# Stick-breaking attention on one core: steps taken in pairs, with the PSUM banks shared out anew

## The chip, the cores and the metric

The kernel runs on one core of a Trainium2 chip. The metric is the device time of one launch in microseconds (us), lower is better. A core has TensorE (PE, with its weight loads as PEld), VectorE (DVE), ScalarE (ACT), GpSimd (POOL) and SyncE (SP, whose queue issues all DMAs here). The TensorE clock has two levels, 1.2 and 2.4 GHz. PSUM is used as eight banks of 128 x 512 float32.

## What is computed

One sequence of 1024 tokens, width 1024, float32, goes through a Mamba-2 layer, a projection to shared K and V, and a stick-breaking attention layer, with a final norm. The change lies in the attention layer, whose reference is, for each of 16 heads of 64 columns and each block of 128 queries:

```python
z = einsum('bthd,bshd->bhts', q[:, lo:hi], k[:, :hi]) * scale
log_keep = where(mask, log_sigmoid(-z), 0)
after = cumsum(log_keep, reverse=True) - log_keep
a = exp(where(mask, log_sigmoid(z) + after, -inf))
o = einsum('bhts,bshd->bthd', a, v[:, :hi])
...
x = x + gate * ((o * silu(z_gate)) @ out_w)
```

The mask is strictly causal. `q` and `z_gate` are projections of the same normed stream, and `k`, `v` come from the stage before.

## The kernel before, in words

All earlier stages (Mamba-2, its output projection, K and V) end at about 982 us of the profile and aren't touched by the change, but for the pool of their projection banks. The attention stage works on eight head pairs `p`. PE's order there is written out by hand (`manual_schedule`, line 897); the other engines' orders are set by a planner, which sees each instruction's inputs and a priority in the order of the program.

**A step** is one row block `i` of 128 queries against up to 512 keys (`c` says which half of the keys), or two smaller ones side by side; nine steps (`order`, line 916) make a head pair, 72 the stage. A step has these parts:

- **S**, `scores` (line 824): six matmuls for each piece (three float32r products for each of two heads, on 64 rows each) into a tile `sc` of two banks. ACT makes two sigmoids of it (`kp` at 836, `be` at 837), POOL masks the diagonal block (843), DVE runs a product scan over `kp` for each head (850), POOL multiplies (856). `above` carries the scan from one half of the keys to the next.
- **T**, `transposes` (line 860): eight transposes of `be`, four for each head `a`, into one bank `at` for each head. ACT copies the first head's bank to SBUF (877), DVE the second's (875), into tiles `aT`.
- **A**, `av` (line 879): when both row blocks `2t` and `2t+1` have all their keys, the value products, 8 to 32 matmuls of up to 256 columns, into a bank `av`; DVE multiplies it with the gate (890).
- **F**, the filler: units of three 512-column matmuls (`mm3`) of the projections of the gates (`zproj1`, 16 units for each head pair) and of the next pair's queries (`qproj`, 16 units), then of the output projections (`oproj`, 7 units each), into one bank `mm` for eight (seven) units. Each bank is then emptied: for queries by a cast on ACT (772) and a subtraction on DVE (773), for gates by a sigmoid (787) and a product (788), for `oproj` by one DVE instruction (801). `load_w` (116) loads each weight tile, casts it on ACT (123) and subtracts on POOL (124).

Before the change, a step of the main loop (line 922) emits T of the step three earlier (`LAG`), then half of its filler units (`rates`, 2 to 4 for a step), then any A that became ready a step earlier (`AVD`), S of the new step, and the other half of the filler. The banks: two `mm`, two for `sc`, two `at`, one `av`, one for a constant. `mm` is a pool of the whole kernel. Four filler units of pair 0's gates run ahead of the loop, and output projections 0 to 5 are run with seven of their eight parts, the sixth left open in its bank until the last stage.

Of the kernel before, what the change touches and what calls it, by code (L numbers as in the profile page):

```python
# [31 lines left out]
LAG = 3  # L32
AVD = 1
NPRE = 5
# [18 lines left out]
def tile_trunk(ctx, tc, xT, xN, c, vec, ada0, adar, wxbc, wwave, wdt, wz, wmo, wk, wv, wq, wqz, wso, out):  # L53
# [37 lines left out]
    pmm = pool(ctx, "pmm", bufs=2, space=PSUM)  # L91
# [6 lines left out]

    esw = ctx.enter_context(ExitStack())
# [13 lines left out]
    def mm_tile(name):  # L113
        return pmm.tile([P, HT], F32, tag="mm", name=name)
# [626 lines left out]
    esw.close()  # L741
    weight_pools(ctx, 1, 2, 2)
    pg = pool(ctx, "pg", bufs=2)
    gg, x2p, part = [{}, {}], [], {}
# [12 lines left out]
    with ExitStack() as es:  # L757
        pa = pool(es, "p5", bufs=2)
        pp = pool(es, "pp5", bufs=2, space=PSUM)
        pone = pp.tile([P, 1], F32, name="pone", bufs=1)  # L760
# [16 lines left out]
        def zproj1(p):  # L777
            wh, wl = load_w(wqz[p], f"qz{p}", parts=4, eng=Q)
            szs[p] = [None] * NH
            for hf in (1, 0):  # L780
                sz = pa.tile([P, HT], F32, tag="sz", name=f"qsz{p}_{hf}", bufs=3)
                szs[p][hf] = sz
                ps = mm_tile(f"pqz{p}_{hf}")
                for k in range(ND):
                    mm3(ps, wh[:, k, :], wl[:, k, :], *h1[k][hf], k == 0, k == ND - 1)
                    if k == ND - 1:
                        S.activation(sz, ps, AF.Sigmoid)
                        V.tensor_tensor(out=sz, in0=ps, in1=sz, op=ALU.mult)
                    yield

        def oproj(d):
            if d < NPRE:
                t = pg.tile([P, HT], F32, tag="x2", name=f"x2_{d}", bufs=NPRE)
                Y.dma_start(out=t, in_=x1_d[d][1])
                x2p.append(t)
            wh, wl = load_w(wso[d], f"so{d}", parts=4, eng=Q)
            ps = mm_tile(f"pso{d}")
            for k in range(7):
                mm3(ps, wh[:, k, :], wl[:, k, :], *gg[1][k], k == 0, k == 6 and d < NPRE)
                if k == 6 and d < NPRE:  # L800
                    V.scalar_tensor_tensor(out=t, in0=ps, scalar=mod[:, GA1, d:d + 1], in1=t,
                                           op0=ALU.mult, op1=ALU.add)
                yield
            part[d] = ps, wh, wl
# [19 lines left out]
        def scores(p, step):  # L824
            kd, q = pairs[p][0], qs[p]
            n = f"{p}_{step[0][0]}_{step[0][1]}"
            kp = pa.tile([P, 2, HT + 2], F32, tag="kp", name="kp" + n)
            be = pa.tile([P, 2, HT], F32, tag="be", name="be" + n, bufs=4)
            ps = pp.tile([P, 2, HT], F32, tag="sc", name="sc" + n, bufs=1)
# [30 lines left out]
        def transposes(p, step, be):  # L860
            n = f"{p}_{step[0][0]}_{step[0][1]}"
            for a in range(2):
                ps = pp.tile([P, 4, P], F32, tag="at", name=f"at{n}_{a}", bufs=2)
# [39 lines left out]
        def filler():  # L903
# [6 lines left out]
            for d in range(NPRE + 1):  # L910
# [10 lines left out]
        live, rows, ready = {}, {}, []  # L921
        for n in range(len(steps) + LAG + AVD):
            rate = rates[n % ns]
            m = n - LAG
            now, ready = [r for r in ready if r[0] <= n], [r for r in ready if r[0] > n]
            if 0 <= m < len(steps):
                p, st = steps[m]
                transposes(p, st, live.pop(m))
                for i, c in st:
                    if i % 2 == 1 and c == 0:  # L930
                        ready.append((n + AVD, (p, i // 2, rows.pop((p, i // 2)))))
            for _ in range((rate + 1) // 2):
                next(fl, None)
            for r in now:
                av(*r[1])
            if n < len(steps):
                p, st = steps[n]
                if n % ns == 0:
                    if p < 7:
                        pairs[p + 1] = load_pair(p + 1)  # L940
                live[n] = scores(p, st)
            for _ in range(rate // 2):
                next(fl, None)
# [4 lines left out]
    with ExitStack() as es:  # L948
        pw = pool(es, "p6w")
        pf = pool(es, "p6", bufs=2)  # L950
        pp = pool(es, "pp6", bufs=2, space=PSUM)
        wos = {}
# [17 lines left out]
        keep_w(NPRE + 1)  # L970
# [3 lines left out]
        for hf, c0, c1, ds in ((1, 0, 512, (0, 5, 1, 2, 3, 4, 6, 7)), (0, 0, 256, (6, 7, 0, 1, 2, 3, 4, 5)),  # L974
# [10 lines left out]
            for i, d in enumerate(ds):  # L985
# [8 lines left out]
                if hf == 1 and d == NPRE:  # L994
                    ps = part[d][0]
                elif hf == 1 and d < NPRE:
# [5 lines left out]
                elif hf == 1 and d == NPRE:  # L1002
                    mm3(ps, part[d][1][:, 7, :], part[d][2][:, 7, :], *gg[1][7], False, True)
# [103 lines left out]
```

## Time and profile before

| | us |
|---|---|
| median of 3 runs | 1463.79 |
| lowest and highest | 1463.76, 1465.89 |
| the profiled execution | 1468.16 |
| its span, first to last instruction | 1465.3 |
| attention stage, from the first score matmul to the last transpose | 987 to 1376 |

Engines over the whole span: PE 98%, PEld 77%, DVE 66%, ACT 50%, POOL 36%. PE's busy time is from start to a modelled end, and neighbouring matmuls overlap, so a PE that is always busy can still lose time at the places where one kind of matmul follows another: there the distances from start to start tell more than the busy time.

### The profile page before, as it was taken

How to read it: one execution, taken by the hardware profiler on the slowest of the kernel's cores; microseconds unless marked ns; L12 is line 12 of the kernel's file. 1: busy time of each engine (PE TensorE's matmuls, PEld its weight loads, DVE VectorE, ACT ScalarE, POOL GpSimd, SP SyncE). 2: the span in 40 equal slices, each digit the busy share in tenths (PEclk: the TensorE clock that was granted, in tenths of full speed). 3: DMA queues.
4: the chain of work that ended last, by engine and by line, in shares of the span. 5: the costliest groups of instructions: out<-in, count | busy, mean ns of one | idle time of the engine just before them, and what ended most of it. 6: DMA issues, size and time to landing. Idle time of an engine off the chain costs nothing.

```text
span 1465.3 us, 20960 instructions
## 1 busy us (share of the span) xinstructions
PE 1431.0 (98%) x7772; PEld 1125.0 (77%) x7772; DVE 965.4 (66%) x1212; ACT 734.8 (50%) x1234; POOL 521.8 (36%) x602
## 2 busy tenths in 40 slices
PE   6998999999999999999999999999999999999997
PEld 3777887888777777778888888887777777777797
DVE  5689984544799888985733627516666666667674
ACT  6654535234666666633522424326555555556452
POOL 0011221001555655431011000027666666667532
PEclk9999999999999999999999999999999999999999
DMA  9368875224577766557433546561222121212253
GB/s 355 127 215 300 293 292 178 101 89 142 172 239 237 233 221 216 191 188 276 156 129 112 197 143 214 168 207 38 80 63 75 58 73 59 71 58 80 92 184 113
DMA packets 105445, 235.75 MB, mean 161 GB/s; under 512 B 9344, under 2 KB 40832, under 8 KB 103296
## 3 DMA queue, kind: packets, MB, share of 16 engines
q1 hardware_dynamic: 105344, 234.42, 47.4%
q8 instruction: 61, 1.00, 0.3%
q14 instruction: 40, 0.33, 0.1%
HBM read 188.51 MB, written 45.88 MB: 160 GB/s over the span
## 4 chain that ended last, share of the span: by engine, by line
PE 80%; DVE 2%; DMA 1%; issue 1%; ACT 1%; POOL 0%; DVEq 0%; SPq 0%; POOLq 0%; ACTq 0%
PE av L886 5%; PE sc L833 4%; PE at L865 4%; PE pz L129 4%; PE pz L131 4%; PE pz L130 4%; PE po L131 4%; PE po L130 4%; PE po L129 4%; PE pq L129 2%; PE pqz L129 2%; PE yd L545 2%; PE pq L131 2%; PE pr L131 2%; PE pr L129 2%; PE pr L130 2%
## 5 line engine op out<-in xcount | busy, mean ns | idle before, releaser
L856 POOL TENSOR_TENSOR be<-be,kp 128x1024 f32<-128x1024 f32 (+2 forms) x96 | 163.1, 1699 | 83.1 <-DVE kp L850 73.9
L836 ACT ACTIVATE kp<-sc 128x1024 f32<-128x1024 f32 (+2 forms) x96 | 75.4, 813 | 149.5 <-PE sc L833 113.9
L850 DVE TENSOR_TENSOR_SCAN kp<-kp,pone 128x128 f32<-128x128 f32 (+3 forms) x128 | 96.7, 804 | 64.0 <-POOL kp L843 64.0
L129 PE MATMUL pr<-h0h,hx 128*128 128x512 f32 x336 | 132.6, 395 | 5.6 <-DVE cv L350 3.8
L131 PE MATMUL pr<-h0h,lx 128*128 128x512 f32 x336 | 132.2, 393 | 0.5 <-DVE lx L124 0.5
L130 PE MATMUL pr<-h0l,hx 128*128 128x512 f32 x336 | 132.1, 393 | 0.0
L129 PE MATMUL pz<-h0h,hz 128*128 128x512 f32 x256 | 112.9, 441 | 0.0
L130 PE MATMUL po<-yl,ho 128*128 128x512 f32 x256 | 100.9, 394 | 0.7 <-DVE yl L659 0.7
L131 PE MATMUL po<-yh,lo 128*128 128x512 f32 x256 | 100.0, 391 | 1.3 <-DVE lo L124 1.3
L131 PE MATMUL pz<-h0h,lz 128*128 128x512 f32 x256 | 100.3, 392 | 0.0
L130 PE MATMUL pz<-h0l,hz 128*128 128x512 f32 x256 | 100.0, 391 | 0.0
L129 PE MATMUL po<-yh,ho 128*128 128x512 f32 x256 | 100.0, 391 | 0.0
L515 ACT ACTIVATE lm<-lm,nac 128x128 f32<-128x128 f32 x256 | 78.6, 389 | 40.9 <-POOL lm L512 40.9
L363 POOL TENSOR_TENSOR ar<-ar,crow 128x1024 f32<-128x1024 f32 x12 | 31.0, 2587 | 184.5 <-DMA ar<-adar 157.0
L850 DVE TENSOR_TENSOR_SCAN kp<-kp,ab,pone 128x512 f32<-128x512 f32 x64 | 78.3, 1265 | 24.9 <-ACT kp L836 14.2
L124 POOL TENSOR_TENSOR lq<-rq,hq 128x256 fp32r<-128x256 f32 x32 | 22.5, 734 | 177.8 <-ACT hq L123 177.8
L550 POOL TENSOR_TENSOR sd<-st,eev 128x512 f32<-128x512 f32 x24 | 38.0, 1581 | 130.6 <-ACT st L562 117.9
L512 POOL TENSOR_SCALAR_AFFINE_SELECT lm<-lm 128x1024 f32<-128x1024 f32 x32 | 44.1, 1377 | 112.7 <-DMA lm<-ac_d 105.6
L350 DVE SCALAR_TENSOR_TENSOR cv<-pr,vt,cv 128x1023 f32<-128x1023 f32 (+2 forms) x63 | 80.2, 1276 | 0.9
L129 PEld LDWEIGHTS pr<-h0h,hx 128*128 128x128 f32 x336 | 63.7, 190 | 19.7 <-issue 4.2
L123 ACT CAST ho<-ro 128x1024 fp32r<-128x1024 f32 x32 | 33.6, 1052 | 85.0 <-PE po L130 66.9
L865 PEld LDWEIGHTS at<-ident,be 128*128 128x128 f32 x576 | 67.2, 140 | 10.6 <-DVE aT L875 0.8
(259 smaller groups left out, 3889.3 us busy)
## 6 DMA issues: line engine op xcount, KB each, us to landing
ar<-adar SPq DMA_DIRECT2D x48, 512.0 KB, 5.3
lm<-ac_d SPq DMA_DIRECT2D x32, 512.0 KB, 5.1
rz<-wz SPq DMA_DIRECT2D x32, 512.0 KB, 3.8
ro<-wmo SPq DMA_DIRECT2D x32, 512.0 KB, 3.7
xs_d<-sv SPq DMA_DIRECT2D x24, 512.0 KB, 3.7
rx<-wxbc SPq DMA_DIRECT2D x21, 512.0 KB, 4.5
a<-ada SPq DMA_DIRECT2D x8, 1024.0 KB, 10.1
xg<-xs_d SPq DMA_DIRECT2D x8, 1024.0 KB, 6.5
```

The lines of the kernel that those rows point to most:

```text
L129: E.matmul(ps, wh, xh, start=first, stop=False)
L130: E.matmul(ps, wh, xl, start=False, stop=False)
L131: E.matmul(ps, wl, xh, start=False, stop=last)
L350: V.scalar_tensor_tensor(out=ac[:, i:], in0=ps[:, :T - i], scalar=vv("cw", m * 4 + 3 - i), in1=ac[:, i:], op0=ALU.mult, op1=ALU.add)
L512: Q.affine_select(out=lm, in_=lm, pattern=[[0, HPG], [1, P]], compare_op=ALU.is_ge, fill=-1e30, base=0, channel_multiplier=-1)
L515: S.activation(lm[:, h, :], lm[:, h, :], AF.Exp, bias=nac[:, c, h0_ + h:h0_ + h + 1])
L833: E.matmul(ps[:, a, o:o + w], q[hsl[a], x, i * P:(i + 1) * P], kd[hsl[a], y, HT * c:HT * c + w], start=b == 0, stop=b == 2)
L836: S.activation(kp[:, :, ok:ok + w], ps[:, :, o:o + w], AF.Sigmoid, scale=-0.125)
L850: V.tensor_tensor_scan(out=ka, data0=ka, data1=pone.to_broadcast([P, w]), initial=1.0 if top else above[p, i][:, a, 0:1], op0=ALU.mult, op ...
L856: Q.tensor_tensor(out=be[:, :, o:o + w], in0=be[:, :, o:o + w], in1=kp[:, :, ok + 1:ok + w + 1], op=ALU.mult)
L865: E.transpose(ps[:, j, :], be[:, a, j * P:(j + 1) * P], ident)
L886: E.matmul(ps[hsl[a], cs], vd[:, j, hsl[a]], at[j // 4][:, a, j % 4, cs], start=j == 0, stop=j == nj - 1)
```

## The change

The loop takes two steps at a time. For pair `m` it emits T of step `2(m-2)`, four filler units, T of step `2(m-2)+1`, four filler units, every A that these two T completed, and then S of steps `2m` and `2m+1` back to back. Every ninth pair (`m % 9 == 8`) has no filler at all, and `m = 0` has none either. The bank shares become: one `mm` (a pool of the stage; the earlier and the last stage have their own with two), four for `sc` (two tiles), two `at` that T and A share, one constant. Output projections 0 to 5 all run with seven parts and are emptied; none is left open. The four filler units ahead of the loop fall away. `aT` becomes two tiles of each of two sizes, `sz` has four buffers, `kp` three.

```diff
-LAG = 3
-AVD = 1
-NPRE = 5
+LAG = 2
+NPRE = 6
...
-    pmm = pool(ctx, "pmm", bufs=2, space=PSUM)
+    pm = {}
...
+    esm = ctx.enter_context(ExitStack())
+    pm["mm"] = pool(esm, "pmm", bufs=2, space=PSUM)
...
     esw.close()
+    esm.close()
...
+        pm["mm"] = pool(es, "pmm5", bufs=1, space=PSUM)
...
-                sz = pa.tile([P, HT], F32, tag="sz", name=f"qsz{p}_{hf}", bufs=3)
+                sz = pa.tile([P, HT], F32, tag="sz", name=f"qsz{p}_{hf}", bufs=4)
...
-                mm3(ps, wh[:, k, :], wl[:, k, :], *gg[1][k], k == 0, k == 6 and d < NPRE)
-                if k == 6 and d < NPRE:
+                mm3(ps, wh[:, k, :], wl[:, k, :], *gg[1][k], k == 0, k == 6)
+                if k == 6:
...
-            ps = pp.tile([P, 2, HT], F32, tag="sc", name="sc" + n, bufs=1)
+            ps = pp.tile([P, 2, HT], F32, tag="sc", name="sc" + n)
...
-                        rows[p, t][c] = pa.tile([P, 2, 4, 256], F32, tag="aT", name=f"aT{p}_{t}_{c}",
-                                                bufs=4)
+                        nb = min(2 * t + 2 - 4 * c, 4)
+                        rows[p, t][c] = pa.tile([P, 2, nb, 256], F32, tag=f"aT{nb}",
+                                                name=f"aT{p}_{t}_{c}")
...
-            ps = pp.tile([P, 256], F32, tag="av", name=f"av{p}_{t}", bufs=1)
+            ps = pp.tile([P, 4, P], F32, tag="at", name=f"av{p}_{t}").rearrange("p a b -> p (a b)")[:, 0:256]
...
-            for d in range(NPRE + 1):
+            for d in range(NPRE):
                 yield from oproj(d)
...
-        for _ in range(4):
-            next(fl)
...
-        rates = (4, 4, 4, 4, 2, 4, 4, 3, 3)
...
-        for n in range(len(steps) + LAG + AVD):
-            rate = rates[n % ns]
-            m = n - LAG
...
+        for m in range(len(steps) // 2 + LAG):
+            ready = []
+            rest = 8 if m % ns != 8 else 0
+            for n in (2 * (m - LAG), 2 * (m - LAG) + 1):
+                if n >= 0:
+                    p, st = steps[n]
+                    transposes(p, st, live.pop(n))
+                    for i, c in st:
+                        if i % 2 == 1 and c == 0:
+                            ready.append((p, i // 2, rows.pop((p, i // 2))))
+                if m > 0:
+                    fill(rest // 2)
+            for r in ready:
+                av(*r)
+            for n in (2 * m, 2 * m + 1):
+                if n < len(steps):
+                    p, st = steps[n]
+                    if n % ns == 0 and p < 7:
                         pairs[p + 1] = load_pair(p + 1)
+                    live[n] = scores(p, st)
...
+        pm["mm"] = pool(es, "pmm6", bufs=2, space=PSUM)
```

## Rows read from the trace of the kernel before

**Rows 1.** The page: engines over the span, and the granted clock in 40 slices.

```profile
PE 1431.0 (98%) x7772; PEld 1125.0 (77%) x7772; DVE 965.4 (66%) x1212; ACT 734.8 (50%) x1234; POOL 521.8 (36%) x602
...
PEclk9999999999999999999999999999999999999999
```

**Rows 2.** Busy time, attention stage: stretch, then engine and count; clock, DMA, GB/s.

```profile
983.00:1379.00 396.00, 395.42 (x2573) 290.18 (x2573) 259.56 (x360) 225.61 (x383) 278.87 (x430) 1.00 0.22 71
```

**Rows 3.** Chain that ended last: first step of two successive head pairs (start, us).

```profile
1126.93 1.01 PE sc L833 x12
...
1175.54 1.01 PE sc L833 x12
```

**Rows 4.** Timeline of PE within a step: start, length, engine, line, tile.

```profile
1100.84 0.98 PE L833 MATMUL sc<-kd,q 64*128 64x256 f32 x12
1101.75 0.50 PE L129 MATMUL pq<-h1h,hq 128*128 128x512 f32 x1
...
1107.22 0.40 PE L131 MATMUL pq<-h1h,lq 128*128 128x512 f32 x1
1107.45 1.03 PE L865 MATMUL at<-ident,be 128*128 128x128 f32 x8
1108.24 0.47 PE L129 MATMUL pq<-h1h,hq 128*128 128x512 f32 x1
1108.56 0.39 PE L130 MATMUL pq<-h1l,hq 128*128 128x512 f32 x1
1108.79 0.40 PE L131 MATMUL pq<-h1h,lq 128*128 128x512 f32 x1
...
1109.48 0.40 PE L131 MATMUL pq<-h1h,lq 128*128 128x512 f32 x1
1109.81 0.96 PE L833 MATMUL sc<-kd,q 64*128 64x512 f32 x6
1110.70 0.50 PE L129 MATMUL pq<-h1h,hq 128*128 128x512 f32 x1
1111.04 0.39 PE L130 MATMUL pq<-h1l,hq 128*128 128x512 f32 x1
```

**Rows 5.** Timeline around a value product.

```profile
1114.55 3.46 PE L886 MATMUL av<-aT,vd 128*64 128x256 f32 x32
...
1117.93 0.54 PEld L833 LDWEIGHTS sc<-kd,q 64*128 64x128 f32 x6 [0.17 <-issue]
```

**Rows 6.** Timeline: a query bank filled and emptied.

```profile
977.18 0.39 PE L131 MATMUL pq<-h1h,lq 128*128 128x512 f32 x1
...
977.61 0.59 ACT L772 CAST q<-pq 128x512 fp32r<-128x512 f32 x1 [4.17 <-PE pq L131]
...
978.22 0.69 DVE L773 TENSOR_TENSOR q<-pq,q 128x512 fp32r<-128x512 f32 x1 [3.54 <-ACT q L772]
```

**Rows 7.** Timeline: an output projection's bank filled and emptied.

```profile
1385.76 0.39 PE L131 MATMUL pso<-gh,lso 128*128 128x512 f32 x1
...
1386.19 0.75 DVE L801 SCALAR_TENSOR_TENSOR x<-pso,mod,x 128x512 f32<-128x512 f32 x1 [0.46 <-PE pso L131]
```

**Rows 8.** Timeline: sigmoids of the S of rows 4, and copies after two T.

```profile
1102.56 1.03 PE L865 MATMUL at<-ident,be 128*128 128x128 f32 x8
...
1105.38 0.67 DVE L875 COPY aT<-at 128x512 f32<-128x512 f32 x1
...
1108.09 0.59 ACT L877 COPY aT<-at 128x512 f32<-128x512 f32 x1
...
1110.95 1.03 ACT L836 ACTIVATE kp<-sc 128x1024 f32<-128x1024 f32 x1 [2.27 <-POOL kp L847]
...
1111.33 0.66 DVE L875 COPY aT<-at 128x512 f32<-128x512 f32 x1
...
1111.87 1.02 ACT L837 ACTIVATE be<-sc 128x1024 f32<-128x1024 f32 x1
```

**Rows 9.** Groups by line and shape, attention stage: busy us, mean ns, idle before.

```profile
L850 DVE TENSOR_TENSOR_SCAN kp<-kp,ab,pone 128x512 f32<-128x512 f32 x64 | 78.3, 1265 | 24.9 <-ACT kp L836 14.2 <-POOL lqz L124 10.0 <-issue 0.2
...
L875 DVE COPY aT<-at 128x512 f32<-128x512 f32 x48 | 32.2, 672 | 16.4 <-PE at L865 16.2
```

**Rows 10.** Timeline: first query matmul, and the last V bank emptied.

```profile
971.42 0.39 PE L129 MATMUL pq<-h1h,hq 128*128 128x512 f32 x1
...
973.93 0.69 DVE L733 COPY vs<-pv 128x512 f32<-128x512 f32 x1 [2.98 <-DMA v_d<-vs]
```

More of the change, by code (lines that the diff above doesn't have):

```diff
@@ L113, in mm_tile @@
     def mm_tile(name):
-        return pmm.tile([P, HT], F32, tag="mm", name=name)
+        return pm["mm"].tile([P, HT], F32, tag="mm", name=name)
     def load_w(src, name, shape=(8, P), parts=1, eng=V):
@@ L741, in tile_trunk @@
     esw.close()
+    esm.close()
     weight_pools(ctx, 1, 2, 2)
     pg = pool(ctx, "pg", bufs=2)
-    gg, x2p, part = [{}, {}], [], {}
+    gg, x2p = [{}, {}], []
     def split_g(hf, k, g):
@@ L791, in oproj @@
         def oproj(d):
[L792 to L795, printed above, removed]
+            t = pg.tile([P, HT], F32, tag="x2", name=f"x2_{d}", bufs=NPRE)
+            Y.dma_start(out=t, in_=x1_d[d][1])
+            x2p.append(t)
             wh, wl = load_w(wso[d], f"so{d}", parts=4, eng=Q)
@@ L803, in oproj @@
                 yield
-            part[d] = ps, wh, wl
         def load_pair(p):
@@ L826, in scores @@
             n = f"{p}_{step[0][0]}_{step[0][1]}"
-            kp = pa.tile([P, 2, HT + 2], F32, tag="kp", name="kp" + n)
+            kp = pa.tile([P, 2, HT + 2], F32, tag="kp", name="kp" + n, bufs=3)
             be = pa.tile([P, 2, HT], F32, tag="be", name="be" + n, bufs=4)
-            ps = pp.tile([P, 2, HT], F32, tag="sc", name="sc" + n, bufs=1)
+            ps = pp.tile([P, 2, HT], F32, tag="sc", name="sc" + n)
             for i, c, w, o, _, _ in pieces(step):
@@ L862, in transposes @@
             for a in range(2):
-                ps = pp.tile([P, 4, P], F32, tag="at", name=f"at{n}_{a}", bufs=2)
+                ps = pp.tile([P, 4, P], F32, tag="at", name=f"at{n}_{a}")
                 for j in range(4):
@@ L909, in filler, with fill @@
                 load_gs(1, k)
-            for d in range(NPRE + 1):
+            for d in range(NPRE):
                 yield from oproj(d)
         fl = filler()
-        for _ in range(4):
-            next(fl)
+        def fill(m):
+            for _ in range(m):
+                next(fl, None)
         order = [((6, 1), (0, 0)), ((6, 0),), ((7, 1),), ((7, 0),), ((1, 0), (5, 1)), ((4, 1), (2, 0)),
                  ((4, 0),), ((5, 0),), ((3, 0),)]
-        rates = (4, 4, 4, 4, 2, 4, 4, 3, 3)
         ns = len(order)
         steps = [(p, st) for p in range(8) for st in order]
-        live, rows, ready = {}, {}, []
-        for n in range(len(steps) + LAG + AVD):
-            rate = rates[n % ns]
-            m = n - LAG
[L925 to L939, printed above, removed]
+        live, rows = {}, {}
+        for m in range(len(steps) // 2 + LAG):
[16 more added lines that the diff above has]
+                    if n % ns == 0 and p < 7:
                         pairs[p + 1] = load_pair(p + 1)
-                live[n] = scores(p, st)
-            for _ in range(rate // 2):
-                next(fl, None)
+                    live[n] = scores(p, st)
         for _ in fl:
@@ L968, in finish @@
                 yield
-        keep_w(NPRE + 1)
+        keep_w(6)
         keep_w(7)
@@ L993, in tile_trunk @@
                     Y.dma_start(out=t, in_=x1_d[d][hf][:, c0:c1])
-                if hf == 1 and d == NPRE:
-                    ps = part[d][0]
-                elif hf == 1 and d < NPRE:
+                if hf == 1 and d < NPRE:
                     ps = mm_tile(f"ps{d}_{n}")
@@ L1001, in tile_trunk @@
                     mm3(ps, w7[0][:, d, :], w7[1][:, d, :], *gg[1][7], True, True)
-                elif hf == 1 and d == NPRE:
-                    mm3(ps, part[d][1][:, 7, :], part[d][2][:, 7, :], *gg[1][7], False, True)
                 else:
```

## The prediction, made before the changed kernel was run

> **What bounds the kernel now.** I read the page first: PE is busy 98% of the span at full clock [rows 1]. Then the busy time of the attention stage alone: PE 395 of 396 us, DVE, ACT and POOL at 57 to 70% [rows 2]. So no engine but PE sets the pace there, and PE has no holes. The chain that ended last says the same with a period: a head pair starts every 48.61 us [rows 3], with no wait for another engine between. What remains to be won is in the distances from start to start, for which I read PE's timeline within a step [rows 4]. A filler matmul follows its like after 0.23 us. A gap above that belongs to the change from one kind of matmul to another:
>
> - F to S: 0.33 from the last filler matmul (1109.48) to S, so 0.10 lost.
> - S itself: six matmuls, in concurrent twos, are worth 3 x 0.23 = 0.69, but the filler starts 0.89 after S: 0.20 lost. The second filler matmul comes after 0.34: 0.11 more. S costs 0.41 in all at its two borders.
> - F to T: 0.23, nothing lost. T to F: 0.32 between the first two filler matmuls, 0.08 lost.
>
> The kernel loses 0.41 x 72 = 30 us to S, and that is what the change attacks. What it takes away to do so is slack: two projection banks, an A bank of its own, filler between any two T, and filler between S and T.
>
> **The gain.** Two steps before: 2 x 0.41 + 2 x 0.08 = 0.98. After: F to S once (0.10), S to S, S to T, T to F twice (0.16). S to S is shown nearly: S of two pieces, 12 matmuls of 256 columns, worth the same 0.69, lets the filler start after 0.91 [rows 4], so a second piece costs nothing at its border; I take 0, the bounds being 0 and 0.31. S to T isn't in the trace. Bounds: 0 (T behind F) and 0.31 (F behind S); I take 0.28, nearer the second, since what is lost behind S is S's own end. After: 0.54, so 0.44 saved for each of 36 pairs, 16 us (from 0.1 x 36 = 4 to 0.72 x 36 = 26). The Trainium skill, TensorEngine Tiling (Array Packing), Key Properties, says that a change of tiling mode, not of the tile, drains TensorE. By it S to S is free, and S (64 rows) to T (128) pays the drain, which is 16 us again and shuts out the 26. Value products: each A has 0.17 us of weight-load idling between itself and S [rows 5] on top of its own border; 32 of them become 24 groups, 8 x 0.2 = 1.6 us. **Gain: 17 us.**
>
> **One projection bank.** An emptied bank must be waited for wherever filler would go on. Filling a bank takes eight units, which are the two blocks of a pair, so its border falls behind the second block, and A, S, S, T (at least 0.69 x 2 + 0.28 + 0.8 = 2.5 us) hide the emptying, which takes 1.83 us when its engines are free: the cast starts 0.43 after the last matmul starts, the subtraction ends at 1.73 [rows 6], and 0.1 to restart. If a scan (1.27 us each) stands before the subtraction, the cover is gone and 0.4 to 1.6 is lost; I take none. Four places have no cover:
> - Pair 0's queries run ahead of the loop: between its halves 1.83 - 0.23 = 1.6 us.
> - The output projections have 7 units, so their borders fall inside filler. Five borders; the DVE step starts 0.43 after the last matmul and takes 0.75 [rows 7], 0.1 to restart, less 0.23: 1.05 each, **5 us**. Leaving none open for the last stage moves no matmul: the same three close it there.
> - The queries of pairs 2, 4, 6 end with the second block directly ahead of the S that reads them (no filler in the ninth pair, and no A there), as do pair 0's. S's second piece needs the half that was just emptied: 0.33 + 3 x 0.17 = 0.85 us after the last matmul it is due, the subtraction is there at 1.83: 1.0 each, **4 us**. For odd pairs an A and an S lie between.
> - The stage's bank may lie over a V bank, the last of which is emptied at 974.62, 3.2 us after the first query matmul [rows 10]. Between 0 and 3.2; the first two V banks are free before, so 0 is taken and 3.2 kept.
>
> **Two banks for T and A.** After S, S, T1 comes at 1.7 us from the first S, ends at 2.5, and four units later T2 is due at 5.3. Its banks need T1's copies. On ACT four sigmoids are ahead of the copy: the first starts 1.14 after S starts, the next 0.92 later [rows 4, 8], so the copy starts at 1.14 + 4 x 0.92 = 4.8 and ends at 5.4, plus 0.1: 0.2 late. On DVE the scans of both steps compete with it: two of 1.27 from 2.4 to 4.9, two more to 7.4 if the planner puts them first, then 0.67 for the copy [rows 9]. Before, the copy ended 2.70 and 3.75 us after the T [rows 4, 8]; now it has 3.2 (second half of T2). So a pair loses between 0 and 2.3 us. I take 0.35, ACT's 0.2 and a third of a pair's T in which DVE is half a microsecond late, as at 1111.33: 32 x 0.35 = **11 us** (0 to 74).
>
> **The ninth pairs** (m = 8, 17, 26, 35) have no filler: S, S, T1, T2, A, A, S, S. T2's first bank waits for T1's copy at 5.5, and T1 ended at 2.5: 3.0 us, and A for the banks after T2 about 0.2 more: 3.2 x 4 = **13 us**. If the copies went ahead of the sigmoids it would be 0.8 each (3 us), if behind all scans 5.5 (22 us).
>
> Other edits: `kp`, `sz` and `aT` have at least as many live tiles as the order needs, so no wait; SP issues the same loads (one `x1` load moves from the last stage into this one), POOL the same subtractions, both with ten microseconds of slack at a fifth of the DMA share [rows 2].
>
> **Sum:** -17 + 1.6 + 5 + 4 + 11 + 13 = +17.6 us. The profiled execution's own time is 1468.2, 0.3% above the median; a shift of 1% is the same on either. From the median 1463.8: **1481 us**.
>
> **Rivals.**
> 1. *The copies come in time* (faster). If the planner sets each T's two copies ahead of the second step's sigmoids and scans, the 11 go and the 13 become 3: -3 us. If S to T is also cheaper than taken, up to -13. It decides at the copy's end: under 3.2 us after T1. For it: DVE sat idle for T for 16.2 us in all [rows 9], so it does sometimes run the copy at once. Against: 3.75 us in rows where S wasn't even adjacent. Time 1457.
> 2. *The copies fall behind both scans in half of the pairs*: 16 x 2.3 in place of 11, and 22 in place of 13: +52, 1516 us.
> 3. *S to S costs as much as S to F*: the gain is 5, not 17: 1493.
> 4. *The clock falls.* Before, the clock stays at 1.00 all through the stage [rows 2], where the longest stretch without filler is A and S, 4.3 us [rows 4, 5]. The ninth pairs have some 11 us of T, waits, A and S. At 1.2 GHz their 8 us of matmuls would double: 4 x 8 = 32 us, 1513. The Trainium skill, TensorE: Matmul & The Clock Gate, Part 4, holds that transposes don't count as work for the clock; by that rule this is where it would fall, and no row here shows it.
>
> **How the numbers follow.** Forecast (all waits near what is taken) 0.60, rival 1 0.25, rival 2 0.08, rival 3 0.04, rival 4 0.03. A measurement of this kernel tells apart about 0.2%, 3 us. Of rival 1, 0.05 lies within 3 us, and of the forecast 0.03. Faster 0.20, same 0.08, slower 0.72. The likeliest's own range is 1470 to 1497. The range 1455 to 1500 leaves out rivals 2 and 4 and the lowest of rival 1, some 0.15.
>
> **What would show it.** Right: the granted clock 1.00; S to S start distance 0.69; PE idle before T on ACT and DVE `aT` copies, 4 large ones of 3 us and many under 1; PE idle before filler for L801, five times; the period of two head pairs 99 to 101 us where it was 97.2. Wrong: a period below 97, or T never waiting for a copy (rival 1), or T to F after S without the 0.2 to 0.3 of S's end.

## The result, and the profile after

The changed kernel takes **1504.18 us** (median, 1503.96 to 1507.27) where the kernel before took 1464.84 on the same chip: 1.027 times as long, interval 1.0253 to 1.0287. It is slower, as predicted, but by 39 us instead of 17.6, and 4 us above the top of the range. The profiled execution's span grew from 1465.3 to 1502.6.

The page's engine row and the busy time of the attention stage (columns as in [rows 1, 2]), for the changed kernel:

```profile
PE 1432.7 (95%) x7772; PEld 1134.1 (75%) x7772; DVE 962.9 (64%) x1213; ACT 734.2 (49%) x1234; POOL 513.7 (34%) x602
```

```profile
983.00:1414.00 431.00, 396.67 (x2591) 299.70 (x2590) 258.71 (x361) 224.42 (x380) 273.21 (x426) 0.98 0.20 65
```

Before, PE had 0.6 us of holes in 396 [rows 2]; now it has 34 in 431, and the mean granted clock of the stage is 0.98 instead of 1.00: 431 x 0.02 = 8.6 us, to the accuracy of that digit. Who owns the holes is told by the list of PE's waits (what PE waited at, on what; us in total, times, longest):

```profile
PE at L866 <- DVE aT L877: 22.9, 20, 2.8
PE pso L130 <- DVE x L803: 5.4, 3, 3.1
PE sc L834 <- ACT q L775: 3.8, 4, 1.0
PE pq L130 <- DVE q L776: 1.4, 1, 1.4
PE sc L834 <- DVE q L776: 1.1, 4, 0.3
PE av L888 <- ACT aT L879: 0.9, 3, 0.3
```

These are 35.5 us in 35 waits; before, the same list for the stage has 0.8 us. The waits are of four kinds (T, S behind a query projection, the start, the output projections), and the prediction has a term for each.

**T2 behind filler.** PE's timeline in a steady pair: the last filler matmul, T2 with its wait in brackets, the first filler matmul behind it.

```profile
1135.31 0.39 PE L132 MATMUL pqz<-h1h,lqz 128*128 128x512 f32 x1
1136.24 1.06 PE L866 MATMUL at<-ident,be 128*128 128x128 f32 x8 [0.55 <-DVE aT L877]
1137.06 0.48 PE L130 MATMUL pqz<-h1h,hqz 128*128 128x512 f32 x1
```

Without a wait T starts 0.23 after filler [rows 4], here 0.93. The wait costs 0.70, not the 0.55 in brackets: idle time counts from the end of the matmul before, and the overlap of neighbours is lost as well.

**The ninth pair**, PE and DVE:

```profile
1164.22 1.09 PE L866 MATMUL at<-ident,be 128*128 128x128 f32 x8
1164.59 2.50 DVE L851 TENSOR_TENSOR_SCAN kp<-kp,pone 128x128 f32<-128x128 f32 x4 [0.71 <-POOL kp L844]
...
1167.00 0.67 DVE L877 COPY aT<-at 128x512 f32<-128x512 f32 x1
...
1167.58 2.44 DVE L851 TENSOR_TENSOR_SCAN kp<-kp,ab,pone 128x512 f32<-128x512 f32 x2
...
1167.81 1.06 PE L866 MATMUL at<-ident,be 128*128 128x128 f32 x8 [2.49 <-DVE aT L877]
...
1169.17 4.11 PE L888 MATMUL av<-aT,vd 128*64 128x256 f32 x40 [0.30 <-ACT aT L879]
```

T1's copy stands behind the first step's scans and ahead of the second's, as the forecast had it and not as rivals 1 and 2 had. It is the order of VectorE's queue that counts, and not only its load: in the first pair with filler of head pairs 2, 4 and 6, T2 waits 1.87, and there VectorE itself has stood idle for 3.62 us (to 1086.03 in head pair 2), waiting for POOL's mask (line 844) ahead of the scans behind which the copy is queued; T1 was done at 1084.6.

**The output projections**, the longest of the three waits:

```profile
1394.42 2.33 DVE L851 TENSOR_TENSOR_SCAN kp<-kp,pone 128x512 f32<-128x512 f32 x2 [2.11 <-POOL kp L844]
1394.52 0.40 PE L132 MATMUL pso<-gh,lso 128*128 128x512 f32 x1
...
1396.67 0.66 DVE L877 COPY aT<-at 128x512 f32<-128x512 f32 x1
...
1397.26 0.74 DVE L803 SCALAR_TENSOR_TENSOR x<-pso,mod,x 128x512 f32<-128x512 f32 x1
...
1398.05 0.50 PE L130 MATMUL pso<-gh,hso 128*128 128x512 f32 x1 [3.13 <-DVE x L803]
```

The last matmul into the bank starts at 1394.52 and ends at 1394.92. The step that empties the bank takes 0.74, but stands behind two scans and a copy.

**The clock.** Windows of PE's busy time (stretch, length, PE, PEld, DVE, ACT, POOL, granted clock, DMA share, GB/s):

```profile
1060.00:1064.00 4.00, 1.86 (x16) 1.21 (x12) 3.29 (x6) 3.77 (x6) 3.27 (x10) 0.99 0.00 0
1064.00:1068.00 4.00, 3.65 (x20) 2.74 (x22) 3.22 (x5) 1.19 (x4) 2.71 (x2) 0.58 0.02 4
...
1166.00:1170.00 4.00, 1.89 (x16) 1.47 (x18) 4.00 (x6) 2.65 (x5) 2.92 (x4) 1.00 0.00 0
1170.00:1174.00 4.00, 4.00 (x42) 2.77 (x40) 1.52 (x5) 0.00 (x0) 2.35 (x4) 1.00 0.00 0
...
1394.00:1398.00 4.00, 0.92 (x4) 0.39 (x3) 3.57 (x4) 1.32 (x4) 1.85 (x4) 1.00 0.00 0
1398.00:1402.00 4.00, 3.95 (x15) 3.32 (x15) 0.00 (x0) 0.44 (x1) 3.85 (x5) 0.57 0.00 0
1402.00:1406.00 4.00, 4.00 (x24) 3.41 (x23) 0.84 (x2) 0.73 (x2) 0.00 (x0) 1.00 0.47 135
```

The level of 1.2 GHz is granted five times in the stage: once behind a ninth pair's wait (1064), and four times from 1356 on, about the waits of the last stretch. Each time costs 4 x 0.43 = 1.7 us of work. Two other ninth pairs, with the same wait (1166 shown), keep the full clock. The windows are those of one execution, but the granted clock of the whole span says the same for all: it is 0.987 to 0.989 in the four executions of the changed kernel and 0.990 to 0.996 in those of the kernel before, and 1500 x 0.005 = 7.5 us.

Where the 37 us lie, from the starts of each head pair's first S, the last matmul of the last A and the end of the span (up to the first S the changed kernel takes 2.8 us less, as six filler units that stood there now come later):

| stretch | before | after | more |
|---|---|---|---|
| first S to head pair 2's | 91.2 | 95.8 | 4.6 |
| head pairs 2 and 3 | 97.2 | 102.4 | 5.2 |
| head pairs 4 and 5 | 97.2 | 102.4 | 5.2 |
| head pair 6's S to the last A | 112.3 | 128.7 | 16.4 (with four filler units fewer) |
| last A to the end | 80.3 | 89.2 | 8.9 (with ten units more, 6.9) |

### The profile page after: what moved, and what is told of

Same layout as the page of the kernel before. It is cut to its first block, busy times and chain, and to the rows that moved or that the text cites. A ratio compares the mean times of both kernels' runs of the same rounds, so it can differ in the third digit from the quotient of the medians.

```text
span 1502.6 us, 20922 instructions
## 1 busy us (share of the span) xinstructions
PE 1432.7 (95%) x7772; PEld 1134.1 (75%) x7772; DVE 962.9 (64%) x1213; ACT 734.2 (49%) x1234; POOL 513.7 (34%) x602
## 5 line engine op out<-in xcount | busy, mean ns | idle before, releaser
L866 PE MATMUL at<-ident,be 128*128 128x128 f32 x576 | 79.7, 283 | 23.0 <-DVE aT L877 22.9
L866 PEld LDWEIGHTS at<-ident,be 128*128 128x128 f32 x576 | 63.9, 144 | 46.4 <-issue 26.3
L851 DVE TENSOR_TENSOR_SCAN kp<-kp,ab,pone 128x512 f32<-128x512 f32 x64 | 78.3, 1265 | 23.1 <-ACT kp L837 19.7
L551 POOL TENSOR_TENSOR sd<-st,eev 128x512 f32<-128x512 f32 x24 | 33.9, 1414 | 130.3 <-ACT st L563 118.3
```

What stands on the lines that cost most here:

```text
L551: Q.tensor_tensor(out=sd, in0=st[g].rearrange("p (h k) -> p h k", k=64), op=ALU.mult, in1=eev[:, c, hsl].unsqueeze(2).to_broadcast([P, HPG ...
L851: V.tensor_tensor_scan(out=ka, data0=ka, data1=pone.to_broadcast([P, w]), initial=1.0 if top else above[p, i][:, a, 0:1], op0=ALU.mult, op ...
```

## The experiments

All are edits of the changed kernel unless it is said otherwise. Times are medians; the kernel before ran beside each, at 1464.8 to 1466.9.

### Banks bought with the constant

The scan multiplies with a column of ones that holds a whole PSUM bank. Moving it to SBUF seemed to free a bank at no price. First in the kernel before:

```diff
-        pone = pp.tile([P, 1], F32, name="pone", bufs=1)
+        pone = pa.tile([P, 1], F32, name="pone", bufs=1)
```

> Control: the kernel before, with the scan's constant of ones moved from PSUM to SBUF, which frees a PSUM bank that nothing here uses. If the scan's second operand may lie in either memory, the time stays within 0.2% of before (1464.8) and the scans keep their mean of 1265 ns for 512 columns. If SBUF costs the scan or POOL something, scans or POOL's products grow, and the runs that use the freed bank must be read against this one.

Measured: 1494.9 us, 1.0211 times the kernel before (1.0176 to 1.0245). Groups by shape, kernel before with the constant in SBUF (columns as in [rows 9]):

```profile
L850 DVE TENSOR_TENSOR_SCAN kp<-kp,ab,pone 128x512 f32<-128x512 f32 x64 | 104.0, 1664 | 17.4 <-ACT kp L836 17.0
...
L843 POOL TENSOR_SCALAR_AFFINE_SELECT be<-be 128x256 f32<-128x256 f32 x64 | 46.2, 738 | 0.4 <-ACT be L837 0.4
...
L124 POOL TENSOR_TENSOR lqz<-rqz,hqz 128x256 fp32r<-128x256 f32 x28 | 39.2, 1418 | 0.0
```

The same groups of the kernel before (its scan is in [rows 9], 1265 ns):

```profile
L843 POOL TENSOR_SCALAR_AFFINE_SELECT be<-be 128x256 f32<-128x256 f32 x64 | 25.1, 411 | 6.7 <-ACT be L837 6.6
...
L124 POOL TENSOR_TENSOR lqz<-rqz,hqz 128x256 fp32r<-128x256 f32 x28 | 20.1, 739 | 0.0
```

The scan takes 1664 ns instead of 1265, and POOL's select and subtraction nearly twice as long. The Trainium skill, SBUF — State Buffer, Who interferes with whom, says that a DVE instruction with two SBUF inputs contends with a GpSimd instruction that reads SBUF; the rows agree. It is POOL that makes the difference, and not the memory alone: of the 96 scans of 512 columns in the attention stage, the 16 beside which POOL did nothing took 1191 to 1272 ns, as in the kernel before (1190 to 1282), and the other 80 took 1647 at the median. The bank is worth 30 us where it is. Two experiments give the changed kernel the freed bank, with the constant in SBUF as above: the first as a third `at` bank, the second as a second `mm` bank.

```diff
-            ps = pp.tile([P, 4, P], F32, tag="at", name=f"at{n}_{a}")
+            ps = pp.tile([P, 4, P], F32, tag="at", name=f"at{n}_{a}", bufs=3)
```

> The changed kernel with the constant in SBUF and the freed bank given to T and A (three at banks). Theory of the bank waits: T's second half no longer waits for the copy of the T before it by DVE; of 3.65 us lost behind filler and 3.4 in a ninth pair for two head pairs, at least half goes, 4 x 3.5 = 14 us, and one or two of the late falls of the clock with it: 1488. Rival, two S at once overload ACT and DVE whatever the banks: waits move to the second half of the same T or to A, and the time stays above 1498.

```diff
-        pm["mm"] = pool(es, "pmm5", bufs=1, space=PSUM)
+        pm["mm"] = pool(es, "pmm5", bufs=2, space=PSUM)
```

> The changed kernel with the constant in SBUF and the freed bank given to the projections (two mm banks in the attention stage). Theory: the one bank costs 1.4 us at the start and 1.4, 3.1 and 0.8 us at borders of output projections in the loop, and what the clock loses behind them; the late queries (1.2 us, four times) stay, since there the data are late and not the bank: 1504 - 7 to -12 = 1492 to 1497. Rival, most of the unexplained loss of the last head pairs (10 us beyond the forecast) is this bank: 1488 or less.

Measured: 1549.0 and 1551.3 us (1.0577 and 1.0585), far over both theories. Against the same scan in the old order, the change costs 54 and 56 us. For the question of the banks both are inconclusive; they suggest that the new order bears a slower VectorE worse than the old one.

### The waits of T2, one at a time

Filler for the ninth pair, taken from the two before it:

```diff
-            rest = 8 if m % ns != 8 else 0
+            rest = 8 if m % ns < 7 else 4
```

> The changed kernel with the filler of the last two pairs of nine at four units each in place of eight and none. Theory of the bank waits: T2 comes 1.4 us later behind T1 in both, so the 2.5 to 3.4 us of a ninth pair become about 1.1 in each of two pairs: 4 x 1 = 4 us gained, and the fall of the clock at the first ninth pair goes (1.7 us): 1498. Rival, the stretch without filler itself (clock, drains) costs most: 1490 or less. Second rival: the eighth pair's new waits eat all: 1504.

Measured: 1509.7 us (1.0306, 1.0286 to 1.0326). The waits come back in the pairs that gave units up: T waits 24 times for 23.6 in all, where it was 20 times for 22.9. This is the second rival, with some 5 us on top.

Filler in pair 0 too (e4), which moves all projections one pair ahead:

```diff
-                if m > 0:
-                    fill(rest // 2)
+                fill(rest // 2)
```

> The changed kernel with eight filler units in the first pair of steps too (m = 0), so that all filler runs eight units earlier: the next pair's queries end in the seventh pair of nine and not directly ahead of the S that reads them. Theory of the late queries: the waits of 0.95 + 0.29 us at the S of head pairs 0, 2, 4, 6 go, 4 to 5 us: 1499. Rival, those waits are cover for others (T's copies get that time): the waits at T grow by as much and the time stays at 1504.

Measured: 1503.6 us (1.0253), the rival's time. The waits of S for queries are gone, T waits 13 times for 17.1, and head pairs 2 and 3 take 99.2 instead of 102.4. All of it is given back elsewhere: another border at the start waits 2.4, `pso` waits 9.8 in all instead of 5.4, and T waits once 2.9 for an A's bank, so that the waits are 35 us as before. The clock is lower as well: 0.981 to 0.985 in the four executions, and in the profiled one it falls seven times in the stage.

Both copies on ScalarE, which has no scans:

```diff
-                    if a:
-                        V.tensor_copy(at, ps[:, o:o + m, :])
-                    else:
-                        S.copy(at, ps[:, o:o + m, :])
+                    S.copy(at, ps[:, o:o + m, :])
```

> The changed kernel with both copies of a T on ScalarE. Theory: T2 waits for DVE, because its copy stands behind the scans of both steps; without it T2 behind filler waits 0.2 to 0.5 us for ACT only and the 3.65 us for two head pairs shrink below 2, the ninth pair's 3.4 stays about 3: 4 x 2 = 8 us and one fall of the clock: 1494. Rival, ACT with four sigmoids ahead is as late as DVE: 1504 or more.

Measured: 1499.9 us (1.0225), between theory and rival. T waits 9 times instead of 20, but for 17.4 in all, up to 4.2 at once; both copies of a T now stand one behind the other on ScalarE.

The copies preferred by the planner:

```diff
-                    if a:
-                        V.tensor_copy(at, ps[:, o:o + m, :])
-                    else:
-                        S.copy(at, ps[:, o:o + m, :])
+                    with tc.high_priority():
+                        if a:
+                            V.tensor_copy(at, ps[:, o:o + m, :])
+                        else:
+                            S.copy(at, ps[:, o:o + m, :])
```

> The changed kernel with the planner told to prefer the copies of T over whatever else is ready on ACT and DVE (rival 1 of the prediction, made to happen). Theory: the order of the queues is the cause, so T2's waits behind filler go (3.65 us for two head pairs) and the ninth pair's fall from 3.4 to about 1: 4 x 6 = 24 us, and the falls of the clock that follow waits of 2.5 us (5 to 8 us): 1475. Rival, a T can't be copied sooner because DVE is in the middle of a scan of 1.2 to 2.4 us anyway: 1495 or more.

Measured: 1502.8 us (1.0247), and T waits 20 times for 24.5: nothing moved, the ninth pairs' waits included. So copies ahead of the scans, which is rival 1 of the prediction, stay untried. Why the planner doesn't let a copy pass the scans isn't shown.

### Scores apart

On top of e4, the first S of a pair goes between the first filler block and T2, so that the two S no longer stand side by side:

```diff
+        def score(n):
+            if n < len(steps):
+                p, st = steps[n]
+                if n % ns == 0 and p < 7:
+                    pairs[p + 1] = load_pair(p + 1)
+                live[n] = scores(p, st)
...
-                if m > 0:
-                    fill(rest // 2)
+                fill(rest // 2)
+                if n % 2 == 0:
+                    score(2 * m)
             for r in ready:
                 av(*r)
...
+            score(2 * m + 1)
```

> The kernel of e4 with the first S of a pair moved between the first filler block and T2, the second where it was: scores no longer back to back, all else (banks, lag, filler ahead) as in e4. If adjacency gives what the trace shows (0.30 us a pair) and costs the waits at T2, this loses 11 us at the borders and wins most of the 3.65 us behind filler and some of the ninth pair's: 4 x 4 = 16 less 11, so 1494 beside e4's 1499. Rival, the banks alone are the cause and not the two S at once: as e4 plus 11, 1510.

Measured: 1493.0 us (1.0188, 1.016 to 1.0217), close to the 1494 expected. First the wait of T in e4, then those of T and A now:

```profile
PE at L866 <- DVE aT L877: 17.1, 13, 3.2
```

```profile
PE av L888 <- issue: 5.8, 4, 1.6
PE at L866 <- DVE aT L877: 0.8, 3, 0.3
PE at L866 <- ACT aT L879: 0.8, 3, 0.3
```

T's 17.1 went down to 1.6 (and once 3.0 for an A's bank); in the ninth pairs part of it moved to A, which now waits 5.8. Head pairs 2 and 3 take 97.9, next to the 97.2 of before. So it is the place of the first S that makes T's copies late. The move does two things: it takes one step's sigmoids and scans from ahead of the copies, and it puts 0.9 us of S between T1 and T2. By an estimate the second alone can save no more than 13 x 0.9 = 12 of the 17 us; beyond that the two aren't separated. But 27 us remain. Most of them lie at the start and behind head pair 6, where `pso` waits 7.2 in all, the transpose 3.0 for an A's bank, and the clock falls.

### The one projection bank

Seven units for a pair once the output projections run, so that the bank changes at the end of a block:

```diff
-            rest = 8 if m % ns != 8 else 0
+            rest = 0 if m % ns == 8 else 8 if m < 34 else 7
...
-                    fill(rest // 2)
+                    fill((rest + 1 - n % 2) // 2)
```

> The changed kernel, but from pair 34 on (output projections) a pair takes 4+3 units of filler instead of 4+4, so that each change of the one projection bank falls at the end of a second filler block, where A, S, S and T1 follow. No part of the computation changes. Theory (the one bank is what costs in the last stretch): the three waits of the changed kernel there, 1.43, 3.13 and 0.84 us before the first matmul of pso, go or fall under 0.5 each, and with them some of the four falls of the clock in that stretch, some 1.65 us each: 1504 - 5 - (0 to 6.6) = about 1496, between 1493 and 1500. Rival (the queue of VectorE is what is late, and takes its time from whatever comes next): the waits come back at T2 or A with the same sum, and the time stays within 3 us of 1504.

Measured: 1498.6 us (1.0221, 1.0189 to 1.0254), in the theory's range. No `pso` waits any more (5.4 gone); T waits 23.3 for VectorE, as in the changed kernel, and 1.2 for ScalarE, so little of it came back. What the clock gave back differs from one execution to the next: it was granted at 0.984, 0.988, 0.991 and 0.993, with times of 1501.8, 1503.4, 1495.4 and 1494.4. The profiled execution is the one at 0.984. Its clock falls six times, two of them in the last stretch instead of four, and four (at 988, 1066, 1169 and 1196) ahead of head pair 6, where PE's order is that of the changed kernel, whose clock fell once there. So where and how often the clock falls isn't fixed by the order of the steps.

The kernel before with one projection bank (the eighth left empty, the sixth output projection left to the last stage):

```diff
+        pm["mm"] = pool(es, "pmm5", bufs=1, space=PSUM)
         pone = pp.tile([P, 1], F32, name="pone", bufs=1)
...
-            for d in range(NPRE + 1):
+            for d in range(NPRE):
                 yield from oproj(d)
...
-        keep_w(NPRE + 1)
+        keep_w(5)
+        keep_w(6)
```

> The kernel before, its order of steps, one score tile, LAG 3 and all, with one projection bank instead of two in the attention stage (the eighth bank stays empty) and with the sixth output projection left to the last stage, third bank of the projections not needed. No part of the computation changes. Theory (the single bank is the larger part of the loss): the old order meets the same borders inside filler, at the start about 3, in the steady part 5 borders per head pair of which those inside a block of filler wait, and with output projections 1 to 3 us each with falls of the clock: 1465 + 15 to 35 = about 1488. Rival (the loss is the new order's, the bank alone is cheap because A, T or S of the old order follow most borders): 1465 + 3 to 8 = about 1470.

Measured: **1598.5 us**, 1.0905 (1.0875 to 1.0935), 132 us more and far over theory and rival. Its waits, a border in the timeline, and the stage as a whole:

```profile
PE pqz L131 <- DVE qsz L792: 35.9, 8, 6.1
PE pq L131 <- DVE qsz L792: 20.0, 7, 3.0
PE pq L131 <- DVE q L777: 14.3, 8, 2.0
PE pso L131 <- DVE x L805: 8.6, 3, 3.6
```

```profile
1132.23 2.33 DVE L854 TENSOR_TENSOR_SCAN kp<-kp,pone 128x512 f32<-128x512 f32 x2 [2.09 <-POOL kp L847]
...
1134.47 0.73 DVE L879 COPY aT<-at 128x384 f32<-128x384 f32 x2
...
1135.12 0.68 DVE L792 TENSOR_TENSOR qsz<-pqz,qsz 128x512 f32<-128x512 f32 x1
...
1135.86 0.50 PE L131 MATMUL pq<-h1h,hq 128*128 128x512 f32 x1 [2.83 <-DVE qsz L792]
```

```profile
983.00:1509.00 526.00, 443.37 (x2631) 316.26 (x2631) 262.23 (x362) 225.85 (x380) 275.98 (x426) 0.93 0.16 54
```

These four lines are 79 us of waits, the clock another 526 x 0.07 = 37. Where a bank changes inside filler, the step that empties it queues behind scans and copies, and PE waits 1.8 to 4.5 us in the steady part and 6.1 at most. The changed order has the same single bank and takes 94 us less: it puts A, S, S and T behind nearly every border. It can't spare the borders that it leaves in the open.

Scores apart with the second score tile given up for a second `mm` and a third `at` bank:

```diff
-        pm["mm"] = pool(es, "pmm5", bufs=1, space=PSUM)
+        pm["mm"] = pool(es, "pmm5", bufs=2, space=PSUM)
...
-            ps = pp.tile([P, 2, HT], F32, tag="sc", name="sc" + n)
+            ps = pp.tile([P, 2, HT], F32, tag="sc", name="sc" + n, bufs=1)
...
-            ps = pp.tile([P, 4, P], F32, tag="at", name=f"at{n}_{a}")
+            ps = pp.tile([P, 4, P], F32, tag="at", name=f"at{n}_{a}", bufs=3)
```

> The kernel with the scores of a pair put apart again and filler from pair 0 on (1493.0), with the two banks of the second score tile given back: one score tile, two projection banks, three banks for transposes and value products. No part of the computation changes. Theory (what the order of steps did not explain is the banks): the wait at the start (2.4), those before pso (2.9, 2.4, 0.8, 1.1) and the 3.0 before a transpose on an A's bank go, about 12.5 us, and some of the four falls of the clock with them, 1.65 each: 1493 - 12.5 - (0 to 6.6) = 1474 to 1481, 1477 taken. Rival (the last stretch is slow because VectorE is behind, whichever bank): the waits move and the time stays over 1488.

Measured: **1474.0 us**, 1.0063 (1.0038 to 1.0088), as the theory had it. Its waits and its stage:

```profile
PE sc L834 <- ACT be L838: 7.9, 5, 2.0
PE pq L130 <- DVE pone L764: 3.2, 1, 3.2
```

```profile
983.00:1390.00 407.00, 398.85 (x2622) 298.25 (x2620) 265.43 (x362) 225.61 (x384) 277.57 (x430) 1.00 0.21 70
```

No wait for a copy is left, and for a projection's bank only the first, which lies over the constant's. With them the falls of the clock went, but for one at 1332 and one at 974, right behind the wait for the constant's bank. Three shares changed at once here, so this run alone doesn't say what each bank is worth.

A second projection bank in the changed order itself, with the scan's speed untouched: its second operation passes the product through, so that any PSUM tile can stand as second operand.

```diff
-        pone = pp.tile([P, 1], F32, name="pone", bufs=1)
-        V.memset(pone, 1.0)
-        pm["mm"] = pool(es, "pmm5", bufs=1, space=PSUM)
+        pm["mm"] = pool(es, "pmm5", bufs=2, space=PSUM)
...
-                    V.tensor_tensor_scan(out=ka, data0=ka, data1=pone.to_broadcast([P, w]),
+                    V.tensor_tensor_scan(out=ka, data0=ka, data1=ps[:, a, o:o + w],
...
-                                         op1=ALU.mult)
+                                         op1=ALU.bypass)
```

> The changed kernel with a second projection bank, out of the bank of the scan's constant: the scan's second operation is a bypass, which passes the product through, and its second operand, whose value then doesn't matter, is the score tile itself. No part of the computation changes. Theory (the missing bank is what the last stretch and the start lose): the waits before the first matmul of pq at the start (1.4) and of pso (5.4 in all) go, and with the latter the falls of the clock after pair 34, four at some 1.65; the waits at T2 (22.9 in all) and before S behind a query projection (4.9) stay, since no projection bank is in them: 1504 - 6.8 - 6.6 = about 1491, between 1487 and 1496. Rival (VectorE's queue is behind whichever bank is asked for): T2 or A wait longer in the last stretch, and the time stays over 1499. The score tile is now read until its scan ends: if S has to wait for that, it shows as a wait of S on the scan's line, and as a gain that is missing.

Measured: 1521.1 us (1.0366), slower than without the bank, so the theory failed, and the rival's time came from another cause than the rival's. The scan's group and the waits:

```profile
L849 DVE TENSOR_TENSOR_SCAN kp<-kp,ab,sc 128x512 f32<-128x512 f32 x64 | 78.3, 1265 | 37.0 <-ACT be L836 37.0
```

```profile
PE at L864 <- DVE aT L875: 36.1, 35, 3.6
PE sc L832 <- ACT q L773: 3.8, 4, 1.0
PE at L864 <- ACT aT L877: 3.3, 2, 2.1
```

The scan runs at 1265 ns again, but now it waits for `be`, the second sigmoid of the same tile, which is 0.9 us later than `kp`. The Trainium skill, PSUM — Partial Sum Buffer, PSUM bank collisions raise a hardware error, says that engines have to be kept apart on a bank; the row agrees in so far as the scan waits although no data ties it to `be`. So the edit delayed the scans, and T's copies behind them: 13 and 3 us more of T's waits. T waits 3.6 in each of the first three ninth pairs, and the clock falls at all three. What the bank does can still be read: no `pq` or `pso` waits for a bank, and from head pair 7's first S to the last A it takes 70.0 us where the changed kernel took 77.9, in spite of T's waits. A clean trial of the changed order with two projection banks wasn't found: nine banks would be needed.

The same banks with scores apart (the two edits together):

> The kernel with the scores of a pair put apart and filler from pair 0 on (1493.0 with one projection bank, 1474.0 with two and one score tile), now with two score tiles, two projection banks and two for transposes and value products, by the same bypass in the scan. No part of the computation changes. Theory (with the borders of the projections covered, nothing is late but what the scores and transposes need themselves): the waits of S on the sigmoids of the score tile (7.9 with one tile) and the 3.2 at the start before pq go, so 1474 - 11 = 1463, and what two banks instead of three for transposes cost comes on top, 0.3 + 0.3 per two head pairs and 3.0 once: about 1468, between 1462 and 1474. Rival (four score banks are worth nothing in this order): as with one tile, 1474 or more.

Measured: 1480.0 us (1.0086, 1.0056 to 1.0116), the rival's time. The waits of S are gone, but A waits 2.1 four times behind T2, which it didn't with three `at` banks, and a transpose once 3.2 for an A's bank. With the later scans of the bypass, a second score tile is worth no more here than a third `at` bank; what it would be worth without them isn't shown. Against scores apart with one projection bank (1493.0) only the second bank and the bypass differ, so that bank is worth some 13 us in this order, in spite of the later scans.

At last, scores apart, one score tile, two `mm` (allocated first) and three `at`, with filler in the ninth pair:

```diff
-            rest = 8 if m % ns != 8 else 0
+            rest = {6: (3, 3), 7: (3, 3), 8: (1, 3)}.get(m % ns, (4, 4))
...
-                fill(rest // 2)
+                fill(rest[n % 2])
```

> The kernel with scores apart, one score tile, two projection banks and three for transposes (1474.0), with the projections' banks allocated ahead of the others, so that the first projection doesn't wait for the constant, and the filler of nine pairs spread as 8 six times, 6 twice and 1+3 in the ninth. No part of the computation changes. Theory (the two waits are all of the rest): the 3.2 at the start and the four waits of 1.59 in the ninth pairs go, the one of 2.0 later stays: 1474 - 9 = about 1465, between 1461 and 1470, no different from the kernel before. Rival (the pairs cost something in themselves, or the waits come back at the pairs that give up filler): 1471 or more.

Measured: 1469.2 us, 1.0017 (1.0003 to 1.0031), in the theory's range. Two head pairs take 96.2 us, one less than before. S still waits 3.6 and T 2.1, more than half of it in head pair 7, and the clock falls twice in it. This kernel is slower than the kernel before by 0.4 to 4.5 us. None of the versions beats the kernel before.

## Why the prediction was wrong

The direction and the parts were right; the sum fell short. Point by point:

- **The waits: right.** 11 + 13 for T, 4 for the queries, 1.6 at the start and 5 for the output projections are 34.6 us. The list of waits has 22.9 + 0.9, 4.9, 1.4 and 5.4: 35.5. T's copies ran on VectorE behind the first step's scans, as taken. That the sums agree so well is partly luck: behind filler T waits 13.9 (11 taken) and in the ninth pairs 9.9 with A's part (13 taken), and the 0.2 a pair for ScalarE in the 11 didn't show, as no T waits for ScalarE. Within the 5.4 the working was off: not five borders of 1.05 with a free engine, but 1.43, 3.13 and 0.84, the others covered by matmuls of the last stage.
- **A wait as its idle time: mis-sized.** The prediction added 0.1 to restart. The rows show 0.15 more than the idle time behind filler (0.70 for 0.55) and 0.3 behind T (3.59 from T1 to T2, where 0.79 is T's own distance, for 2.49 of idle). At some 0.2, an estimate from these two, 35 waits are 7 us. The 34.6 holds 0.1 for most of them already. This is also why two head pairs take 102.4 us and not the 99 to 101 that the prediction named.
- **The gain: about as predicted.** Two head pairs have 7.3 us of waits, 1.6 to restart, and are 5.2 longer: 3.7 was won in nine pairs, where 0.44 x 9 + 0.4 = 4.4 was taken. PE's starts in head pairs 2 to 5 (18 pairs), summed by what follows what and with the idle time set apart, give the same without a remainder:

| us, from each part's start to the next part's | before | after |
|---|---|---|
| S | 33.4 | 31.3 |
| filler, beyond 0.2295 for each of its 384 matmuls | 10.9 | 6.6 |
| A | 33.5 | 33.4 |
| T | 28.5 | 31.0 |
| idle time before a matmul | 0.0 | 14.4 |

S and filler take 6.4 less. In the filler's 6.6, 1.9 lie between filler and T2 beyond what a T cost there before; without them S and filler are 8.3 down. T takes 2.5 more, of which 1.0 is the first T's part of the border behind S and 1.5 the late T. So 8.3 + 0.1 - 1.0 = 7.4 were won in 18 pairs, 3.7 in nine, and the late T cost 3.4 beyond their idle time, 1.7 in nine pairs. Of the prediction's signs, S to S is free: two S (1.38 of work) let T start 1.60 after they began, so 0.22 is lost there, and 0.06 more within T (0.85 to the filler instead of 0.79), where 0.28 was taken. The Trainium skill, TensorEngine Tiling (Array Packing), Key Properties, has a drain at a change of mode and not of the tile; these rows agree.

```profile
1173.21 1.66 PE L834 MATMUL sc<-kd,q 64*128 64x512 f32 x12
...
1174.81 0.88 PE L866 MATMUL at<-ident,be 128*128 128x128 f32 x6
```

- **The clock: the step that failed.** The forecast has "the granted clock 1.00" and nothing for it in the sum; rival 4 had 0.03 and looked at the ninth pairs alone. In the profiled execution the clock fell five times, 8 us in all, four of them in the last stretch, where T's waits and those for the projection bank come close together; over all executions its share is 7.5 us. In rival 4's place, the first three ninth pairs, it fell once behind waits of 2.5 us, and it fell at all three in the runs where T waits 2.8 (copies on ScalarE) and 3.6 (four score and two projection banks). The Trainium skill, TensorE: Matmul & The Clock Gate, Part 4, says that a transpose in TensorE's transpose mode doesn't count as busy in the same way as other matmuls; in the ninth pairs transposes and waits come together, so the rows neither bear it out nor rule it out.
- **The end.** Ten filler units were left for behind the last A, and this part grew by 2 us more than their own time.

Sum: -15 (four stretches at 3.7), +35, +7, +8, +2 = +37, the growth of the span. So of the 20 us that were missing, 8 are the clock and 7 the restarts; the rest are small ones. Rivals 1 to 3 did not happen; of rival 4 a quarter came, and mostly elsewhere. The clock's share is read from its rows. It goes with the waits in three kernels (a stage's mean of 1.00 with 8 us of idle time in it, 0.98 with 34, 0.93 with 83), but not in step: filler in pair 0 has the same 35 us of waits as the changed kernel and a lower clock in every execution. What makes the clock fall at one wait and not at another stays open, and a trial that keeps the waits and holds the clock up was not made.

The range's upper end of 1500 failed by 4 us. It took in larger waits of T, but neither a falling clock nor waits that cost more than their idle time; without either of the two the time would lie inside it (1496 or 1497, an estimate from the terms above).

What is shown by experiment: moving the first S away from the second takes most of T's waits and 10.5 us (scores apart against e4); a second projection bank is then worth some 13 us, and 132 in the old order; and with scores apart and the banks given back nearly all of the loss is gone (1469.2). Not shown by experiment are what one projection bank costs in the changed order itself, and where in the last stretch each microsecond went, which is read from rows.

## What to carry to other kernels

A PSUM bank that only lets one engine run ahead of another is worth what stands in the other's queue when the bank is full, not the length of the instruction that empties it: 0.7 us of work cost waits of 1.8 to 4.5. Borders removed on a saturated PE win tenths of a microsecond each; one wait costs more than several of them, and more than its idle time, since overlap and sometimes the clock are lost with it. Before a bank is moved, list what fills and empties at each of its changes, and look at the last stretch by itself.

## What was not expected of the hardware

A constant of one column is worth a PSUM bank: as second operand from SBUF it made the scan 1.3 times as long (1265 to 1664 ns) and POOL's work up to 1.9 times (739 to 1418), while the scans beside which POOL stood idle kept their time. And a scan whose second operand is a PSUM tile that ScalarE is still reading waited for ScalarE, though neither writes it; whether the chip needs that or only the planner's waits impose it, no run here tells.
